# Zero-tile matmuls on TensorE ahead of and between the first transposes of an MLP kernel

## The chip, the cores and the metric

One core of a Trainium2 chip (trn2). The metric is device time in microseconds (us) of one execution, lower is better.

## The reference

A two-layer perceptron over 8192 tokens; the kernel computes in fp16 with fp32 accumulation.

```python
# x (8, 1024, 1024), w1 (1024, 4096), w2 (4096, 1024), all float32
def reference(x, w1, w2):
    h = x @ w1
    h = 0.5 * h * (1 + np.tanh(np.sqrt(2 / np.pi) * (h + 0.044715 * h ** 3)))
    return (h @ w2).astype(np.float32)
```

## The kernel before

Tokens are worked on in 8 superblocks of 1024 (`sb`). Each matrix product is split into 2x2 blocks and done with seven block products (Winograd's form of Strassen's scheme) instead of eight, so many operands are sums of blocks, made on DVE. In the first superblock everything has to be brought in: x arrives in fp32 and is transposed on TensorE; weights arrive in fp32 and are cast to fp16 by ACT and POOL.

```python
    def tt(out, in0, in1, op):                      # every sum on DVE comes from here (L111)
        nc.vector.tensor_tensor(out=out, in0=in0, in1=in1, op=op)
    # ... cut ...
        def load_cols(self, c, n):                  # first quad of w1, by columns
            cs = slice(c * P, (c + n) * P)
            kn = 2 * KH // n
            for b in range(2):
                cast = (nc.scalar.copy, pool_copy)[b]
                # ... cut: load fp32 weights into "gc", then cast(...)  (ACT L186, POOL L122)
    # ... cut ...
    def x_first():
        identity = consts.tile([P, P], F32, name="identity")
        make_identity(nc, identity)
        blocks = x_blocks()
        xs = XOps(blocks)
        for a in (1, 0):
            for q in range(NQ):
                # ... cut: load a [128 x 1024] fp32 tile xn of x
                for k in (1, 0):
                    ps = psum()
                    for j in range(KH):
                        nc.tensor.matmul(ps[:, j * P:(j + 1) * P],            # L244
                                         lhsT=xn[:, k, j * P:(j + 1) * P], rhs=identity,
                                         is_transpose=True, start=(j == 0), stop=(j == KH - 1))
                    # ... cut: copy ps to fp16, on DVE for k == 0, on ACT for k == 1 (L253)
            if a:
                xs.make(2)
        return xs
```

The first product, `matmul1`, runs seven products of four matmuls for each of 16 columns `c`. The same PSUM bank serves several products, with DVE and ACT reading it in between:

```python
        for c in range(NI):
            q, j = divmod(c, QC)
            # ... cut
            pb, qb = psum(), psum()
            product(pb, w, 4, True, False)          # each product: four 128x512 matmuls (L288)
            v = temp()
            nc.scalar.copy(out=v, in_=pb)           # L354
            product(qb, w, 5, True, False)
            u = temp()
            tt(u, v, qb, SUB)
            if late is not None:
                finish(*late)                       # product 6 of the column before
            rb = psum()
            product(rb, w, 1, True, False)
            s = temp()
            tt(s, u, rb, ADD)                       # must be read before product 7 adds to rb
            product(pb, w, 2, False, True)
            gelu("21", c, pb)                       # L298, ACT
            s2 = temp()
            tt(s2, s, pb, SUB)
            product(qb, w, 3, False, False)
            gelu("12", c, qb)
            product(rb, w, 7, False, True)
            # ... cut
            if j:
                ahead(q + 1, j)                     # operand sums of the next quad of columns
```

In the first two superblocks `ahead` makes the operand sums of the next quad on DVE, in steps:

```python
        def ahead(q, step):
            # ... cut: for sb > 1 the finished operands are loaded instead
            if step == 0:
                quad = MadeQuad(q, sb == 0)         # sb == 1: loads the blocks from raw_d
                quads.append(quad)
                # ... cut
            for m in ((), (4,), (1, 3), (7, 6))[step]:
                quads[q].sum(m)                     # one tt of 128x2048, then a store
            # ... cut
```

A scheduler orders the instructions of each engine when the program is built. In the first columns it puts products 4 and 5 of the second column ahead of product 3 of the first.

Of the kernel before, what the change touches and what calls it, by code (L numbers as in the profile page):

```python
# [9 lines left out]
DT = mybir.dt.float16  # L10
# [4 lines left out]
P = 128  # L15
# [41 lines left out]
def kernel(  # L57
# [7 lines left out]
    nc = tc.nc  # L65
# [3 lines left out]
    _, I = w1.shape  # L69
    _, O = w2.shape  # L70

    SB = 1024
    HT = SB // 2
# [4 lines left out]
    NQ = HT // P  # L78
# [9 lines left out]
    consts = ctx.enter_context(tc.tile_pool(name="consts", bufs=1))  # L88
# [12 lines left out]
    def psum():  # L101
        return pp.tile([P, HT], F32, name="ps")
# [4 lines left out]
    def unit(rows, cols):  # L107
        return up.tile([P, rows, cols], DT, name="u")
# [4 lines left out]
    def flat(t):  # L113
        return t.rearrange("p a b -> p (a b)")
# [3 lines left out]
    def load_in_order(out, in_, **kw):  # L118
        return tc.keep_in_program_order(nc.sync.dma_start(out=out, in_=in_, **kw))
# [108 lines left out]
    def x_blocks():  # L228
        return {b: unit(KH, HT) for b in ("22", "21", "12", "11")}

    def x_first():
        identity = consts.tile([P, P], F32, name="identity")
        make_identity(nc, identity)
        blocks = x_blocks()
        xs = XOps(blocks)
        for a in (1, 0):
            for q in range(NQ):
                r0 = a * HT + q * P
                xn = up.tile([P, 2, HT], F32, name="u")
                load_in_order(flat(xn), x2[r0:r0 + P, :])  # L240
# [3 lines that stand above are left out]
                        nc.tensor.matmul(  # L244
                            ps[:, j * P:(j + 1) * P],
                            lhsT=xn[:, k, j * P:(j + 1) * P],
                            rhs=identity,
                            is_transpose=True,
                            start=(j == 0),
                            stop=(j == KH - 1),  # L250
                        )
                    eng = nc.vector.tensor_copy if k == 0 else nc.scalar.copy
                    eng(  # L253
                        out=blocks[f"{a + 1}{k + 1}"][:, :, q * P:(q + 1) * P],
                        in_=ps.rearrange("p (j t) -> p j t", t=P),
                    )
            if a:
                xs.make(2)
        return xs
# [282 lines left out]
    def matmul2(sb, g):  # L542
# [69 lines left out]
                last = store(sb, b, q, c)  # L612
        return last

    warm = consts.tile([P, 1], F32, name="warm")
    nc.vector.memset(warm, 0.0)
    nc.scalar.activation(out=warm, in_=warm, func=GELU)
    xs = x_first()
    for sb in range(NSB):
        g, quad = matmul1(xs, sb)  # L620
# [39 lines left out]
```

## Time and profile before

| | |
|---|---|
| time, median of the first 3 runs | 1597.25 us (1596.09 to 1597.75) |
| span of the profiled run | 1593.6 us |
| TensorE (PE) busy | 1562.5 us, 98% |
| TensorE idle before 34 us | about 10 us |
| TensorE idle at 237 to 281 us | 9.0 us, in four waits |

The page of the profile of before gives busy time by engine and the chain that ended last: TensorE is the bottleneck as a whole.

```profile
PE 1562.5 (98%) x7872; PEld 774.8 (49%) x7872; DVE 945.6 (59%) x1203; ACT 485.2 (30%) x804; POOL 184.6 (12%) x270
...
PE 79%; DMA 2%; DVE 2%; issue 1%; ACT 0%; SPq 0%; DVEq 0%
```

The timeline of TensorE of before has the start, the length, and in brackets how long the engine was idle ahead of the entry and what ended that. Runs of matmuls without a pause are merged into one line.

```profile
4.42 5.58 PE L244 MATMUL ps<-identity,u 128*128 128x128 f32 x32 [4.42 <-DMA u<-in_x_dram]
...
17.62 1.04 PE L288 MATMUL ps<-u 128*128 128x512 f16 x4 [2.45 <-DVE u L111]
19.77 8.75 PE L288 MATMUL ps<-u 128*128 128x512 f16 x27 [1.12 <-POOL u L122]
29.30 4.26 PE L288 MATMUL ps<-u 128*128 128x512 f16 x19 [0.77 <-DVE tmp L111]
33.74 86.57 PE L288 MATMUL ps<-u 128*128 128x512 f16 x398 [0.18 <-DVE tmp L111]
...
244.81 32.48 PE L288 MATMUL ps<-u 128*128 128x512 f16 x136 [6.11 <-DVE tmp L111]
279.58 1.02 PE L288 MATMUL ps<-u 128*128 128x512 f16 x4 [2.30 <-DVE tmp L111]
```

After the transposes TensorE waits 2.45 and 1.12 us, then works with one short wait, and from 33.74 us it runs for 86.6 us without one. The two longest waits of the rest of the program end at 244.81 and 279.58 us (a wait of 2.16 us for a load ends at 1532.73 us).

The table of stretches of before, for TensorE (start:end, length, busy time and, in brackets, the matmuls that fall wholly or partly into the stretch, granted clock as a share of full speed, DMA share, GB/s; DMA packets are counted by their start, so that a share can read over 1):

```profile
18.00:20.00 2.00, 0.88 (x5) 0.64 1.19 294
20.00:22.00 2.00, 2.00 (x6) 0.50 1.03 311
22.00:24.00 2.00, 2.00 (x6) 0.50 1.09 371
24.00:26.00 2.00, 2.00 (x8) 0.66 0.97 289
```

The granted clock falls to 0.50 within the first line and comes back within the last; finer slices put the two changes at 18.55 and 25.38 us. At 20 to 24 us TensorE is busy all the time, with six matmuls in a stretch of 2 us.

Around it, the timeline of DVE and ACT of before:

```profile
19.75 6.20 DVE L111 TENSOR_TENSOR u<-u 128x512 f16<-128x512 f16 x11 [1.06 <-POOL u L122]
...
25.11 0.60 ACT L298 ACTIVATE g<-ps 128x512 f16<-128x512 f32 x1 [4.08 <-PE ps L288]
...
25.61 1.98 ACT L186 CAST u<-gc 128x1024 f16<-128x1024 f32 x2
25.88 0.67 DVE L111 TENSOR_TENSOR tmp<-tmp,ps 128x512 f32<-128x512 f32 x1
...
27.62 1.03 DVE L111 TENSOR_TENSOR u<-u 128x1024 f16<-128x1024 f16 x1 [1.06 <-ACT u L186]
...
28.57 0.68 DVE L111 TENSOR_TENSOR tmp<-tmp,ps 128x512 f32<-128x512 f32 x1
...
29.17 1.28 DVE L111 TENSOR_TENSOR u<-u 128x1024 f16<-128x1024 f16 x2
```

DVE makes eleven operand sums in one unbroken piece of 6.20 us. In its queue, the subtraction at 25.88 us comes after them and the addition at 28.57 us after another sum, which waits for two weight casts on ACT (25.61 us), which stand in ACT's queue behind a gelu (25.11 us), which waited for TensorE. TensorE's wait before 29.30 us is for that addition.

### The profile page before, as it was taken

How to read it: one execution, taken by the hardware profiler on the slowest of the kernel's cores; microseconds unless marked ns; L12 is line 12 of the kernel's file. 1: busy time of each engine (PE TensorE's matmuls, PEld its weight loads, DVE VectorE, ACT ScalarE, POOL GpSimd, SP SyncE). 2: the span in 40 equal slices, each digit the busy share in tenths (PEclk: the TensorE clock that was granted, in tenths of full speed). 3: DMA queues.
4: the chain of work that ended last, by engine and by line, in shares of the span. 5: the costliest groups of instructions: out<-in, count | busy, mean ns of one | idle time of the engine just before them, and what ended most of it. 6: DMA issues, size and time to landing. Idle time of an engine off the chain costs nothing.

```text
span 1593.6 us, 20478 instructions
## 1 busy us (share of the span) xinstructions
PE 1562.5 (98%) x7872; PEld 774.8 (49%) x7872; DVE 945.6 (59%) x1203; ACT 485.2 (30%) x804; POOL 184.6 (12%) x270
## 2 busy tenths in 40 slices
PE   7999998999999999999999999999999999999998
PEld 4444443444444455444554445544555445544455
DVE  6863245644755576555675557656475556655564
ACT  4644213431044301442114410244103430044200
POOL 2230113001310012000120001200012001200000
PEclk9999998999999999999999999999999999999999
DMA  9998999663994456845677346954469545663164
GB/s 305 349 297 292 274 388 357 188 241 115 359 320 133 185 223 246 273 104 198 245 273 233 115 178 245 331 184 171 154 244 364 153 163 198 243 244 133 53 223 173
DMA packets 169090, 365.22 MB, mean 229 GB/s; under 512 B 73120, under 2 KB 79264, under 8 KB 168096
## 3 DMA queue, kind: packets, MB, share of 16 engines
q1 hardware_dynamic: 152128, 297.84, 53.3%
q0 software_dynamic: 16864, 66.07, 12.6%
q8 instruction: 61, 1.00, 0.2%
q14 instruction: 37, 0.30, 0.1%
HBM read 285.21 MB, written 93.32 MB: 238 GB/s over the span
## 4 chain that ended last, share of the span: by engine, by line
PE 79%; DMA 2%; DVE 2%; issue 1%; ACT 0%; SPq 0%; DVEq 0%
PE ps L288 42%; PE ps L556 32%; PE ps L503 6%; DMA u<-w_d 1%; DVE u L111 1%; DMA u<-raw_d 1%; DVE tmp L111 0%; DMA u<-in_d 0%; DVE gc L111 0%; ACT tmp L585 0%; SPq L386 0%; DVEq L111 0%; SPq L492 0%
## 5 line engine op out<-in xcount | busy, mean ns | idle before, releaser
L288 PE MATMUL ps<-u 128*128 128x512 f16 x3584 | 782.2, 381 | 13.7 <-DVE tmp L111 9.9
L288 PEld LDWEIGHTS <-u 128*128 128x128 f16 x3584 | 351.9, 98 | 441.5 <-issue 19.8
L111 DVE TENSOR_TENSOR tmp<-tmp,ps 128x512 f32<-128x512 f32 x548 | 375.6, 687 | 312.7 <-ACT tmp L354 121.7
L556 PE MATMUL ps<-u,gc 128*128 128x512 f16 x1472 | 320.0, 379 | 0.0
L298 ACT ACTIVATE g<-tmp 128x512 f16<-128x512 f32 x256 | 161.1, 630 | 295.1 <-DVE tmp L111 295.1
L556 PEld LDWEIGHTS <-gc 128*128 128x128 f16 x1472 | 144.1, 98 | 173.6
L556 PE MATMUL ps<-u,g 128*128 128x512 f16 x896 | 195.7, 379 | 0.0
L111 DVE TENSOR_TENSOR u<-u 128x2048 f16<-128x2048 f16 (+2 forms) x130 | 133.8, 1067 | 87.8 <-ACT u L141 42.9
L298 ACT ACTIVATE g<-ps 128x512 f16<-128x512 f32 x256 | 152.2, 596 | 97.5 <-PE ps L288 97.3
L111 DVE TENSOR_TENSOR u<-u,ps 128x512 f32<-128x512 f32 x152 | 101.3, 682 | 83.3 <-ACT tmp L593 37.3
L386 POOL DMA_DIRECT2D out_dram<-tmp x72 | 39.2, 545 | 901.1 <-ACT tmp L585 723.8
L556 PEld LDWEIGHTS <-g 128*128 128x128 f16 x896 | 87.7, 98 | 104.4
L406 PE MATMUL ps<-u,g 128*128 128x512 f16 x512 | 111.2, 379 | 2.5 <-ACT tmp L451 2.5
L111 DVE TENSOR_TENSOR gc<-g,g 128x2048 f16<-128x2048 f16 x92 | 109.4, 1222 | 6.5 <-PE ps L556 6.5
L503 PE MATMUL ps<-u,gc 128*128 128x256 f16 x960 | 111.0, 274 | 0.8
L354 ACT COPY tmp<-ps 128x512 f32<-128x512 f32 x128 | 73.0, 570 | 104.0 <-PE ps L288 104.0
L503 PEld LDWEIGHTS <-gc 128*128 128x128 f16 x960 | 94.6, 99 | 13.4 <-issue 1.9
L111 DVE TENSOR_TENSOR gc<-u 128x2048 f16<-128x2048 f16 x60 | 73.2, 1220 | 39.2 <-PE ps L556 39.2
L111 DVE TENSOR_TENSOR tmp<-ps,tmp 128x512 f32<-128x512 f32 x128 | 88.4, 691 | 6.6 <-PE ps L288 1.9
L406 PEld LDWEIGHTS <-g 128*128 128x128 f16 x512 | 50.1, 98 | 63.4 <-issue 3.5
L111 DVE TENSOR_TENSOR u<-tmp,ps 128x512 f32<-128x512 f32 x28 | 19.3, 688 | 91.7 <-PE ps L556 80.4
L585 ACT COPY tmp<-ps 128x512 f32<-128x512 f32 x28 | 16.4, 587 | 177.3 <-PE ps L556 177.3
(33 smaller groups left out, 415.6 us busy)
## 6 DMA issues: line engine op xcount, KB each, us to landing
u<-w_d SPq DMA_DIRECT2D x316, 512.0 KB, 8.0
u<-in_d SPq DMA_DIRECT2D x84, 512.0 KB, 7.7
gc<-in_w_dram SPq DMA_DIRECT2D x64, 512.0 KB, 7.2
out_dram<-tmp POOLq DMA_DIRECT2D x72, 256.0 KB, 3.8
xb<-in_x_dram POOLq DMA_DIRECT2D x56, 256.0 KB, 11.2
w_d<-u SPq DMA_DIRECT2D x28, 512.0 KB, 6.5
w_d<-u POOLq DMA_DIRECT2D x28, 512.0 KB, 8.7
out_dram<-u POOLq DMA_DIRECT2D x40, 256.0 KB, 6.5
```

The costliest lines, as they stand in the source:

```text
L111: nc.vector.tensor_tensor(out=out, in0=in0, in1=in1, op=op)
L288: nc.tensor.matmul(bank, lhsT=ops[m][:, k, cs], rhs=xs[m][:, k, :], start=(first and k == 0), stop=(k == KH - 1), skip_group_check=not first,)
L298: gelu_last[0] = nc.scalar.activation(out=g[b][:, c, :], in_=src, func=GELU)
L354: nc.scalar.copy(out=v, in_=pb)
L386: return queue.dma_start(out=out2[r0:r0 + P, o0:o0 + OH], in_=src)
L406: nc.tensor.matmul(banks[i], lhsT=g[f"{i // NQ + 1}{a + 1}"][:, c, (i % NQ) * P:(i % NQ + 1) * P], rhs=w[a], start=(c == 0 and a == 0), st ...
L503: nc.tensor.matmul(bank[:, i * HO:(i + 1) * HO], lhsT=t[:, c, i * P:(i + 1) * P], rhs=y[j][:, c, :], start=(first and i == 0 and c == 0), ...
L556: nc.tensor.matmul(banks[q], lhsT=a[:, c, :], rhs=pieces[c // QC][:, c % QC, :], start=(first and c == 0), stop=(c == NI - 1), skip_group_ ...
L585: nc.scalar.copy(out=c21, in_=ps)
```

## The change

Intent: in before TensorE is idle for most of the time from 15.2 to 18.5 us, and its clock reads 0.50 from 18.55 to 25.38 us. Matmuls on a zero tile, whose result nobody reads, should keep it busy from the first microsecond and between the transposes, so that the transposes and the first real matmuls find the full clock.

```diff
+    def keep_clock(bank, n):
+        for _ in range(n):
+            tc.keep_in_program_order(
+                nc.tensor.matmul(bank, lhsT=idle[:, :P], rhs=idle, start=True, stop=True)
+            )
+
     def x_first():
         identity = consts.tile([P, P], F32, name="identity")
         make_identity(nc, identity)
+        idle_bank = psum()
+        keep_clock(idle_bank, 8)
         blocks = x_blocks()
@@ after the transposes and copies of each x tile @@
+                keep_clock(idle_bank, 2 if a or q < NQ - 1 else 6)
             if a:
                 xs.make(2)
@@ at the start of the program @@
+    idle = consts.tile([P, HT], DT, name="idle")
+    nc.vector.memset(idle, 0.0)
```

The program gains 28 matmuls (8, then 7 times 2, then 6) and one memset. The order of all other instructions on every engine, compared with the buffers' names mapped onto each other, is the same.

## The prediction

> **What bounds the kernel.** TensorE: the busy list gives PE 1562.5 us of 1593.6 (98%), the chain of waits ends 79% on PE. After 285 us the stage table shows PE full. The fillers touch the first 30 us. There, by timeline and half-microsecond windows:
>
> - 4.42 to 15.17 us: 64 fp32 transposes, fed by x tiles that land about every 1.3 us (DMA share 1.0). A transpose record averages 424 ns at 4 to 6 us and 276 ns at 12 to 14 us, the pitch going from about 0.21 to 0.133 us near 8.4 us: the array starts slow, although the clock column reads 1.00 there.
> - The clock column reads 0.50 from 18.6 to 25.35 us. Matmuls at 19.77 to 25.3 us stand 427 ns apart instead of 216.
> - [...]
>
> **What the change does.** Instruction order is otherwise identical. It adds 28 matmuls 128x512 (8 before the transposes, 2 after each of seven x tiles, 6 after the last), one small DVE memset, and holds one of 8 PSUM banks during the transposes. Costs (estimates from the spacings above): 28 x 0.216 = 6.0 us warm, up to twice that cold. The first 8 (about 3.4 us cold) fit almost wholly into the wait for x, ending about 4.6 us instead of 4.42. Then each tile costs 8 x 0.133 + 2 x 0.216 = 1.50 us on PE, more than the 1.3 us of its load: the transposes turn PE-bound and end at about 16.5 to 17.8 us, not 15.17, depending on when the clock rises.
>
> **How much is critical.** Twelve matmuls between 19.77 and 24.9 us gain about 2.5 us if warm. But PE's next product needs an operand sum on DVE, which runs without a pause from 19.75 to 25.95 us; it is ready only at about 24.6 us. So PE will wait from 22.3 to 24.6; most of the gain becomes idle time. What remains is indirect: gelu of the first product runs near 22.4 instead of 25.11 us, ACT's weight casts behind it (25.61 before) start about 1.5 us sooner, so do DVE's sum at 27.62 and the add that ends PE's wait at 29.30 us. Worth about 1.4 us. Later transposes push DVE's chain back 0.3 to 1.5 us, and the new wait at 22 to 24.6 us may let the clock fall again. Net at 34 us: 0.7 us sooner, give or take 1.5. PE is full from 34 to 122 us, and the loads of 125 to 280 us follow gelu, so I expect most of it to survive.
>
> **Prediction.** 1596.5 us, range 1594 to 1599.5; faster by over 2%: 0.01, within 2%: 0.98, slower: 0.01.
>
> **Signs.** Right: transposes at their short pitch before 8 us; last transpose after 16 us; clock 1.00 at 18.6 to 22 us; first products 216 ns apart; PE idle before the second column's first product, waiting for DVE; gelu near 22.5 us; everything after 34 us shifted by one constant, about a microsecond. Wrong: transposes still ending near 15.2 us, or clock 0.50 at 19 us.
>
> **What would break it.** [...]switching between fp32 transposes and fp16 fillers costing more than the sum; the stall at 238.7 to 244.8 us changing length; run-to-run spread (1596.09 to 1597.75) as large as the effect.

The sum came to 0.7 us sooner at 34 us, give or take 1.5.

## The result, and the profile after

| | before | changed |
|---|---|---|
| median of 4 runs | 1596.71 us (1596.09 to 1597.75) | 1596.28 us (1595.5 to 1598.14) |
| ratio | | 1.0002, 95% interval 0.9988 to 1.0016 |
| span of the profiled run | 1593.6 us | 1594.2 us |
| PE busy | 1562.5 us | 1567.3 us |

A ratio is the mean time of one kernel's fast runs over that of the other's fast runs of the same rounds, so it is not quite the ratio of the medians. The ratio in this table is that of before over changed, as the means show, 1596.82 and 1596.55 us; in the experiments below it is the kernel's time over that of before. Medians and means differ by 0.4 and 0.3 us in favour of the change, well inside the interval: no difference is shown. The page of the changed kernel:

```profile
PE 1567.3 (98%) x7900; PEld 775.8 (49%) x7900; DVE 948.7 (60%) x1204; ACT 485.0 (30%) x804; POOL 184.1 (12%) x270
```

The timeline of TensorE of the changed kernel (line numbers are 9 to 10 higher than in before; L235 is a filler). Entries that follow without a pause, the transposes and the other fillers among them, are left out, and so is the one at 90.10 us.

```profile
1.19 3.59 PE L235 MATMUL ps<-idle 128*128 128x512 f16 x8 [1.19 <-DVE warm L628]
...
18.33 1.04 PE L298 MATMUL ps<-u 128*128 128x512 f16 x4 [1.16 <-DVE u L111]
20.35 4.45 PE L298 MATMUL ps<-u 128*128 128x512 f16 x12 [0.98 <-POOL u L122]
25.25 7.70 PE L298 MATMUL ps<-u 128*128 128x512 f16 x34 [0.45 <-DVE u L111]
33.70 10.21 PE L298 MATMUL ps<-u 128*128 128x512 f16 x46 [0.75 <-DVE tmp L111]
44.67 44.93 PE L298 MATMUL ps<-u 128*128 128x512 f16 x205 [0.77 <-ACT tmp L364]
...
244.42 31.93 PE L298 MATMUL ps<-u 128*128 128x512 f16 x136 [5.26 <-DVE tmp L111]
279.76 20.50 PE L298 MATMUL ps<-u 128*128 128x512 f16 x86 [3.41 <-DVE tmp L111]
```

TensorE now has no pause from 1.19 to 17.17 us. Then it waits as before: 1.16 us for the first operand, 0.98 us for a POOL cast, and then 0.45 us for a sum on DVE. The unbroken piece of work starts at 33.70 us, where before it started at 33.74. And it is not unbroken any more: there are waits of 0.77 us before 44.67 and 0.50 us before 90.10 us. The two long waits are there too, 5.26 and 3.41 us.

The table of stretches of the changed kernel:

```profile
18.00:20.00 2.00, 1.04 (x4) 1.00 1.19 301
20.00:22.00 2.00, 1.65 (x5) 0.62 0.96 274
22.00:24.00 2.00, 2.00 (x7) 0.53 1.01 337
24.00:26.00 2.00, 1.55 (x8) 1.00 1.02 326
```

The clock was held past 18.55 us, where it fell before, but it fell at 20.47 us and came back at 23.89 us. The DVE and ACT timeline of the changed kernel:

```profile
20.33 6.21 DVE L111 TENSOR_TENSOR u<-u 128x512 f16<-128x512 f16 x11 [0.51 <-POOL u L122]
...
24.84 0.60 ACT L308 ACTIVATE g<-ps 128x512 f16<-128x512 f32 x1 [3.56 <-PE ps L298]
...
25.33 1.98 ACT L186 CAST u<-gc 128x1024 f16<-128x1024 f32 x2
...
27.35 0.69 DVE L111 TENSOR_TENSOR u<-u 128x1024 f16<-128x1024 f16 x1 [0.22 <-ACT u L186]
...
27.95 0.68 DVE L111 TENSOR_TENSOR tmp<-tmp,ps 128x512 f32<-128x512 f32 x1
...
28.55 1.53 DVE L111 TENSOR_TENSOR u<-u 128x1024 f16<-128x1024 f16 x2
```

The piece of eleven sums starts 0.6 us later than before and is as long; the gelu and the casts are 0.3 us earlier; the addition that TensorE waits for is 0.6 us earlier (27.95 for 28.57). By 33.7 us nothing is left of that.

### The profile page after: what moved, and what is told of

It is laid out like the page before. It is cut to its first block, busy times and chain, and to the rows that moved or that the text cites. A ratio compares the mean times of both kernels' runs of the same rounds, so it can differ in the third digit from the quotient of the medians.

```text
span 1594.2 us, 20535 instructions
## 1 busy us (share of the span) xinstructions
PE 1567.3 (98%) x7900; PEld 775.8 (49%) x7900; DVE 948.7 (60%) x1204; ACT 485.0 (30%) x804; POOL 184.1 (12%) x270
## 4 chain that ended last, share of the span: by engine, by line
PE 88%; DMA 7%; DVE 2%; ACT 1%; issue 1%; SPq 1%; POOL 0%; DVEq 0%; ACTq 0%
PE ps L298 46%; PE ps L566 32%; PE ps L513 6%; PE ps L416 3%; DMA gc<-in_w_dram 3%; DMA u<-w_d 2%; DVE u L111 1%; DMA u<-raw_d 1%; DMA w_d<-u 1%; ACT u L141 1%; SPq L119 0%; DMA u<-in_d 0%; DVE tmp L111 0%; DVE gc L111 0%; DMA u<-in_x_dram 0%
```

## The experiments

Every kernel below gave correct results. Time marks come from one profile each; the times from 5 or 6 runs a kernel. How coarse a mark is shows in the first stage: it ends (first matmul of the second product) at 120.2, 121.1, 122.4, 120.8 and 121.0 us in the five profiles of programs that work alike up to there, without fillers at the start (two of them have one memset more). The start of the long piece of work, which is TensorE's 51st product matmul, is as coarse: 33.74, 32.39, 34.52, 33.65 and 33.30 us in the same five, and 34.53 us in the profile of probe28, whose fillers come later.

Theory A: the first 34 us are paced by the sums on DVE and by weight loads, so the clock of TensorE there is worth next to nothing. Theory B: the clock was worth 2.5 us, but these fillers stop too early to hold it.

### The changed kernel again

> The changed kernel once more, unaltered. Theory A (the first matmuls are paced by the operand sums on DVE and by the weight loads, so their clock is worth next to nothing): total within 1 us of before. It also shows how far the time marks of one and the same kernel scatter. In the first profile of it the clock fell to 0.50 at 20.4 us and the second half of the first stage (first matmul of matmul2_first) began at 121.8 us, against 120.2 before. If those 1.6 us belong to the change, they come again; if they are chance, this mark lands anywhere between 119.5 and 122 us.

Measured: 1595.28 us median of 5 (1594.37 to 1596.48), before 1597.08 us (11 runs); ratio 0.9992, interval 0.998 to 1.0004. The end of the first stage came at 121.0 us, not 121.8; both lie inside what programs without the fillers show (120.2 to 122.4), so the 1.6 us of the first profile cannot be put down to the change. More telling: in this profile the clock did not fall at all in the first 36 us. Two stretches of it:

```profile
22.00:24.00 2.00, 0.52 (x3) 1.00 1.08 347
24.00:26.00 2.00, 0.94 (x5) 1.00 0.40 100
```

With the clock at 1.00, the 12 matmuls are done by 22.5 us, and then TensorE does nothing for 2.54 us. The timeline of TensorE of the same run:

```profile
25.06 7.69 PE L298 MATMUL ps<-u 128*128 128x512 f16 x34 [2.54 <-DVE u L111]
33.72 10.16 PE L298 MATMUL ps<-u 128*128 128x512 f16 x46 [0.97 <-DVE tmp L111]
```

The same kernel had a slow clock for 3.4 us in one run and none in another, and both times the long piece of work started at 33.7 us. That fits theory A, though one such mark proves little.

### No fillers between the transposes, 14 at the end (nm14)

```diff
-                keep_clock(idle_bank, 2 if a or q < NQ - 1 else 6)
+                keep_clock(idle_bank, 0 if a or q < NQ - 1 else 14)
```

> Fillers before the first transpose (8) and after the last (14), none between; the order of all other instructions is unchanged. Transposes should end near 15.0 us again, fillers run until about 18.2 us, and the clock should stay 1.00 through 16 to 23 us. Theory A: the matmuls from 19.7 to 22.3 us then run at full clock, TensorE waits until about 24.6 us for the sum on DVE, and the total stays within 0.8 us of before. Theory B (the fillers of the change stop too early, and a held clock would bring the 2.5 us that the slow matmuls cost): total 2 to 3 us under before and the mark of 120.2 us at about 117.7. The recorded prediction: about 1.4 us, by way of gelu and ACT's weight casts starting sooner.

Measured: 1595.94 us (1593.75 to 1596.28); ratio 0.9993, interval 0.9981 to 1.0005. The clock was 1.00 from 14 to 36 us. TensorE waited 2.13 us for a sum before 24.05 us, as theory A has it, and its long piece started at 33.09 us, 0.65 us sooner than before:

```profile
24.05 7.59 PE L298 MATMUL ps<-u 128*128 128x512 f16 x34 [2.13 <-DVE u L111]
33.09 86.76 PE L298 MATMUL ps<-u 128*128 128x512 f16 x398 [1.45 <-DVE tmp L111]
```

Theory B, which asked for 2 to 3 us, falls by the profile: the clock was held, TensorE waited for DVE all the same, and the first stage ended at 119.7 us, not near 117.7. (The total alone would not exclude 2 us.) The 0.65 us lie inside the scatter of that mark, and DVE's eleven sums began 0.62 us sooner in this profile as well (19.13 us), behind a POOL cast that had its weights sooner, so they are not shown to be the clock's. A cost that the prediction did not have shows in two lines of the timeline of this kernel, of DVE and of POOL:

```profile
27.66 2.13 DVE L111 TENSOR_TENSOR u<-u 128x1024 f16<-128x1024 f16 x2 [0.34 <-POOL u L122]
27.86 2.84 POOL L122 CAST u<-gc 128x1024 f16<-128x1024 f32 x2 [0.23 <-DMA gc<-in_w_dram]
```

The addition was 1.92 us sooner than before, the pair of 128x1024 sums 1.5 us sooner. But there it met two POOL casts, and took 2.13 us instead of 1.28; the casts took 1.42 us each instead of 1.04. In before POOL was idle for nearly all of that pair. Both records are longer while they run side by side; what the two contend for, the trace does not show.

### 14 at the end, with the fillers in between (last14)

```diff
-                keep_clock(idle_bank, 2 if a or q < NQ - 1 else 6)
+                keep_clock(idle_bank, 2 if a or q < NQ - 1 else 14)
```

> The changed kernel with 14 instead of 6 fillers after the last transpose, order otherwise unchanged. Transposes end at 15.9 us as in the changed kernel, fillers run to about 18.8 us, clock 1.00 until at least 23 us. Theory A: total within 0.8 us of before, DVE's long run of sums starts about 0.5 us later than before (20.3 against 19.75). Theory B: 2 us under before. If the delayed transposes are what eats a gain, this one is about 0.5 us slower than the version without fillers between the transposes.

Measured: 1595.52 us (1593.45 to 1597.36); ratio 0.9993, interval 0.9981 to 1.0005, the same as nm14. Here the clock held until 25.55 us and then fell until 28.96 us, after TensorE's new wait for DVE from 22.3 to 24.45 us. So four profiles with fillers had three different clocks (low at 20.5 to 23.9, low at 25.5 to 29.0, twice never low), and one time, within the scatter. Two expectations were missed: the last transpose ended at 15.08 us, not 15.9, and DVE's sums began at 19.53 us, not 20.3. So in this profile the transposes were not delayed, and it says nothing of what a delay costs.

### A known cost in the first stage (probe28)

```diff
+    def fill(bank, n, after):
+        with tc.issue_after(after.ins):
+            for _ in range(n):
+                last = tc.keep_in_program_order(
+                    nc.tensor.matmul(bank, lhsT=idle[:, :P], rhs=idle, start=True, stop=True)
+                )
+        return last
@@ in matmul1; product() now returns its last matmul, and the idle tile is made as in the change @@
             pb, qb = psum(), psum()
+            if sb == 0 and c == 12:
+                fill(pb, 28, p2)         # 28 zero-tile matmuls, placed after product 2 of c == 11
             product(pb, w, 4, True, False)
```

> Before, with 28 filler matmuls of 216 ns (6.05 us by the spacing of before) put in front of one product at about 95 us, where TensorE is busy without a pause; order otherwise unchanged. If a time gained or lost by TensorE in the first stage reaches the end in full, the total is 6.0 us over before, and the mark of 120.2 us becomes 126.2. If the loads of 125 to 280 us set the pace there and take up such shifts, the total is under 3 us over before.

Measured: 1600.73 us (1600.15 to 1603.66); ratio 1.003, interval 1.0018 to 1.0042, which is 4.8 us of 1597, between 2.9 and 6.7. The fillers are worth 6.05 us. So about four fifths of what TensorE loses late in the first stage reaches the end, between a half and all of it by the interval. The mark came at 128.1 us, not 126.2: 1.9 us too late, which is no more than the scatter of this mark. That a gain at that point would show as a loss does is argued, not shown; by their marks the kernels with fillers had none beyond the scatter to pass on.

### POOL's early casts moved to ACT, without and with a held clock (actcast, actcast_nm14)

```diff
-                cast = (nc.scalar.copy, pool_copy)[b]
+                cast = pool_copy if b and c == 0 else nc.scalar.copy
```

> Before, with one change: the weight casts of columns 1 to 3 that POOL did (two of 128x512 at 21.2 us, two of 128x1024 at 25.6 and 27.1 us) are done by ACT, which waits in that stretch; no fillers, so the slow clock from about 18.6 to 25.35 us stays. If the sums on DVE (11 from 19.75 to 25.95 us, mean 456 ns for a 128x512) are long because POOL casts run beside them, the same sums take 0.5 to 1 us less. With the clock low TensorE is not ready for them, so the total stays within 1 us of before.

> The same move of casts from POOL to ACT, with the 8 and 14 fillers of the version without fillers between the transposes, so that the clock is held at 1.00. Theory A, refined: once the clock is held, DVE sets the pace, and half of what it wins is lost again because its pair of 128x1024 sums runs beside POOL casts (2.13 us against 1.28 in the profile of before). Without those casts the pair takes about 1.3 us again, TensorE's unbroken stream starts at 31.9 to 32.6 us (33.09 with POOL casts, 33.74 before), and the total is 1 to 2 us under before. If DVE is not what paces it, the stream starts at 33.1 us as without the move.

Measured: actcast 1596.15 us (1594.62 to 1597.32), ratio 1.0006, interval 0.9994 to 1.0019; actcast_nm14 1596.18 us (1593.69 to 1597.04), ratio 1.0003, interval 0.999 to 1.0015; before, 1595.31 us (9 runs). The eleven sums took 5.38 us instead of 6.20 in both, so POOL's casts had cost them 0.8 us. With the clock held too, the pair of sums was short again. DVE of actcast_nm14, and TensorE of it:

```profile
27.35 1.29 DVE L111 TENSOR_TENSOR u<-u 128x1024 f16<-128x1024 f16 x2
```

```profile
32.53 10.16 PE L298 MATMUL ps<-u 128*128 128x512 f16 x46 [1.00 <-DVE tmp L111]
43.13 26.65 PE L298 MATMUL ps<-u 128*128 128x512 f16 x121 [0.44 <-ACT tmp L364]
```

The long piece started at 32.53 us, 1.2 us sooner than before and within the expected 31.9 to 32.6. In actcast, where the clock was low from 19.80 to 23.22 us, it started at 32.93 us, so the held clock is worth 0.40 us of this, and the mark scatters by 2 us. The collision is shown for this pair, though the pair after it, at 29.16 us, met POOL's next cast and took 2.13 us in its turn. The expected 1 to 2 us of total did not come: at 43.13 us TensorE waited 0.44 us for ACT's copy of a PSUM bank, and the first stage ended at 120.1 us, against 120.2 before (in actcast at 121.6). In ACT's queue that copy stands behind a cast that sat idle 1.88 us for weights from DRAM, in this run and, with 1.36 to 2.49 us, in the others. I read this as the weight loads taking back what the first 33 us win; the copy behind the cast is shown, but that the loads could not have come sooner is not. Nor does this wait account for all of it: the matmul that ends it was still 0.85 us ahead of the same one in before (43.13 and 43.98 us), and where the rest went between 44 and 120 us is open.

### Fillers in the long wait at 239 us (stall24)

```diff
-            product(qb, w, 3, False, False)
+            p3 = product(qb, w, 3, False, False)
+            if sb == 1 and c == 0:
+                fill(psum(), 24, p3)
```

> Before, with 24 fillers (5.2 us) in the long wait of TensorE at 238.7 to 244.8 us, where the clock falls to 0.50 and stays there until 250.7 us; nothing at the start of the program. If a filler pays where TensorE itself is what the next work waits for, the clock stays 1.00, the 14 slow matmuls after the wait go at 216 ns instead of 427, and the mark of 343.0 us (first matmul of the next stage) and the total come 2 to 3 us sooner. If the loads that end TensorE's next wait (at 277 to 280 us) set the pace, that wait grows by the same 2 to 3 us and the total stays within 0.8 us of before.

Measured: 1595.68 us (1594.97 to 1596.72), before 1595.31 us; ratio 1.0004, interval 0.9991 to 1.0018. This is the clean form of the question, because here the clock costs more (in before it was low for 10.24 us, from 240.42 us, against 6.83 us from 18.55 us): one stretch of before, then the same stretch of stall24.

```profile
246.00:248.00 2.00, 2.00 (x6) 0.50 1.03 418
```

```profile
246.00:248.00 2.00, 2.00 (x11) 1.00 1.02 414
```

At half clock six matmuls fall into these 2 us, with the clock held eleven. All of it was given back at TensorE's next wait, which was 2.30 us before (for an addition behind a sum that had waited 4.52 us for a load) and is now 5.29 us (in that wait the clock fell, and it was low from 280.26 to 283.68 us):

```profile
280.48 19.72 PE L296 MATMUL ps<-u 128*128 128x512 f16 x83 [5.29 <-DVE tmp L111]
```

The expected alternative came true. The load that this sum waits for was issued 2.1 us sooner than before (264.86 and 266.95 us), but it landed 0.9 us later (277.92 and 277.02 us), and the next stage began at 345.2 us, against 343.0 before. One load of x on POOL's queue also went ahead of a store here; what that did to the loads was not tried.

### The wait itself: sums behind the subtraction (unblock)

In before, DVE's queue at 239 us holds a sum for a later quad, waiting 5.30 us for a load, ahead of the addition that TensorE needs (244.07 us). DVE of before:

```profile
242.93 1.23 DVE L111 TENSOR_TENSOR u<-u 128x2048 f16<-128x2048 f16 x1 [5.30 <-DMA u<-raw_d]
244.07 1.46 DVE L111 TENSOR_TENSOR tmp<-tmp,ps 128x512 f32<-128x512 f32 x2
```

```diff
             for m in ((), (4,), (1, 3), (7, 6))[step]:
-                quads[q].sum(m)
+                if sb == 1 and q > 1:
+                    with tc.issue_after(s2_last[0].ins):   # the subtraction of the current column
+                        make_sum(quads[q].ops, m, quads[q].raw, KH, QW)
+                    nc.gpsimd.dma_start(out=w1_d[q][:, m - 1, :], in_=flat(quads[q].ops[m]))
+                else:
+                    quads[q].sum(m)
```

> Before, without fillers; in the second superblock the sums of the third and fourth quad on DVE are issued after the subtraction of the current column, because one of them, waiting 5.3 us for a load, stands in DVE's queue ahead of the addition that TensorE waits for at 238.7 us. If that order causes the 6.1 us wait, it shrinks to under 1 us, the clock does not fall at 240.5 us, and the mark of 343.0 us comes 3 to 9 us sooner, less what the wait at 277 to 280 us takes back. If the load itself is needed by the next column anyway, the wait only moves and the total stays within 1 us.

Measured: 1588.84 us (1587.45 to 1591.7), before 1595.31; ratio 0.9964, interval 0.9951 to 0.9976. Run again: 1591.25 us (1590.73 to 1592.53), before 1596.31; ratio 0.9971, interval 0.9959 to 0.9984.

> The reordered sums once more, as the partner of the next two: 5 to 8 us under before. In its first profile TensorE waited 4.76 us at 239.7 to 244.45 us, with the clock at 0.50 from about 243 to 249 us, and then not at all until 339.5 us.

The gain is real, but the expected reason is half wrong. The wait at 239 us did not shrink to under 1 us; it was 4.76 and 5.16 us in the two profiles, because behind the load stood another hold-up. TensorE and DVE of unblock:

```profile
244.45 95.10 PE L288 MATMUL ps<-u 128*128 128x512 f16 x428 [4.76 <-DVE tmp L111]
```

```profile
243.71 0.69 DVE L111 TENSOR_TENSOR tmp<-tmp,ps 128x512 f32<-128x512 f32 x1 [5.10 <-DMA out_dram<-tmp]
```

The addition now waits 5.10 us for a store of an earlier result, whose buffer it is to write. What went away is the wait at 280 us, where a sum waiting for a load had stood in the same way: after 244 us TensorE does not wait again until the next stage. The rest came from the wait at 239 us, shorter by 1.0 to 1.4 us, and from the slow clock after it, which lasted 6.8 us instead of 10.2. The next stage began 3.6 and 4.3 us sooner than before, within the expected 3 to 9. (The wait for the store was not tried further.)

### Fillers, once the next wait is gone (unblock_stall20, unblock_nm14)

The edit of stall24 with 20 fillers, and the edit of nm14, each on top of unblock.

> The reordered sums, with 20 fillers (4.3 us) in TensorE's wait of 4.76 us at 239.7 us. The same kind of filler gained nothing in the order of before, because the next wait, for loads at 277 to 280 us, grew from 2.3 to 5.3 us. Here that wait is gone, so the held clock should now reach the end: 13 matmuls at 216 instead of 427 ns, 2 to 2.8 us under the reordered sums alone (1586 to 1587 us if those take 1588.8). If a loads-bound wait comes back near 280 us, the two take the same time within 0.8 us.

> The reordered sums together with the fillers at the start (8 before, 14 after the transposes), that is the change's idea in its better form in a kernel that waits less. Theory A: whatever the first 33 us win (0.65 us in one profile) is less than the scatter that the weight loads put on the first stage (its end lay between 119.7 and 122.4 us in all profiles), so within 0.8 us of the reordered sums alone. If the old waits at 240 to 280 us were what swallowed the gain of the start, it shows here as 1 us or more.

Measured, in the same rounds as the second run of unblock (1591.25 us): unblock_stall20 1589.33 us (1588.11 to 1592.26), ratio to before 0.9961, interval 0.9947 to 0.9975; unblock_nm14 1590.31 us (1589.58 to 1593.16), ratio 0.9968, interval 0.9955 to 0.998. The means of five are 1591.4, 1589.7 and 1590.8 us. In the profile of unblock_stall20 the clock stays at 1.00:

```profile
246.00:248.00 2.00, 2.00 (x11) 1.00 1.04 422
```

TensorE of the same run, after the fillers:

```profile
244.32 92.80 PE L296 MATMUL ps<-u 128*128 128x512 f16 x428
```

The next stage begins at 337.0 us, against 339.4 and 338.7 us with the reordered sums alone, and TensorE has no wait in between. So the fillers that gained nothing before gain 1.7 us in the means here, a little under the expected 2 to 2.8; the intervals overlap, so the totals alone would not prove it, and the marks, 1.7 to 2.4 us apart, carry the scatter of the stages before. What supports it best is the length of this piece: from the first matmul after the wait to the next stage it takes 94.9, 95.0 and 94.9 us in unblock, its second run and unblock_nm14, where the clock is low for 6.8 us, and 92.6 us here. The fillers at the start change nothing beyond the scatter here either (0.6 us in the means, stage ends 121.1 and 120.8 us), so it was not the old waits at 240 to 280 us that hid their gain.

unblock_stall20 has the lowest ratio of the kernels tried, 0.39% under before.

## Why the prediction was right or wrong

The prediction's time, range and verdict were right: 1596.5 us predicted, 1596.28 us measured, no difference to before shown. There is luck in that: the range is 5.5 us wide, and no effect at all would have fallen into it too. Its small net gain of about 0.7 us is within what the runs cannot tell apart. Step by step:

- **TensorE would wait for DVE once its matmuls were fast.** Right, and the core of it. Predicted: idle from 22.3 to 24.6 us. Measured where the clock held: idle from 22.5 to 25.06 us (the changed kernel, again) and from 21.9 to 24.05 us (nm14). This wait is where the 2.5 us went. One distance shows it: from the start of DVE's eleven sums to TensorE's 17th product matmul, the one that ends this wait, it is 4.91 or 4.92 us in nine profiles, with and without fillers, however long the clock was low. In the profiles of before and probe28 it is 5.12 us, so at this point the slow clock had cost 0.20 us and no more. Shorter sums move it: 4.09 us in actcast_nm14.
- **Transposes end at 16.5 to 17.8 us.** Wrong; the last ended at 15.88 us. The failed term is the "8 x 0.133" of a tile. The 0.133 us came from dividing the length of a group of eight, 1.06 us, by eight; but that length holds the whole record of the last one, 0.273 us, while the starts stood 0.109 us apart. Tiles followed each other 1.305 us apart, so after 0.43 us for two fillers, eight transposes take 0.87 us. They were busy without pause all the same, and the delay was 0.7 us. Even that came with the slow start. In before the starts of the first 19 transposes stood 0.213 us apart (the first two 0.239 us), and 0.109 us within a group of eight from 8.41 us on, with the clock column at 1.00 throughout. In last14, with the same fillers in between, the transposes stood 0.109 us apart from 5.1 us on, in the changed kernel only from 7.0 us, and in last14 the last one ended at 15.08 us.
- **Clock 1.00 at 18.6 to 22 us.** Not in the first profile (down at 20.47 us), yes in the second. That the clock differs from run to run should have been the expectation. The fillers end at 17.2 us. In the first profile waits of 1.16 and 0.98 us for DVE and POOL follow; in the second it had one wait of 1.57 us. How busy TensorE must be for the clock to hold is not shown.
- **Gelu near 22.5 us, casts 1.5 us sooner, the addition sooner.** Right when the clock held: gelu at 22.56 us, first cast at 23.45 us for 25.61, addition at 27.76 us for 28.57.
- **"Worth about 1.4 us", net 0.7 us at 34 us.** Not shown. The changed kernel had 0.04 and 0.02 us at the start of its long piece, its best form 0.65 us, and all of it lies inside the scatter of that mark without fillers, 32.39 to 34.53 us. A term that the sum lacked is the collision of DVE's sums with POOL's casts, 0.85 us on one pair (2.13 for 1.28 us). That it ate the gain is not shown: with those casts taken away the held clock brought 0.40 us (actcast_nm14 against actcast), less than the 0.65 us with them.
- **"I expect most of it to survive."** Not decided. In actcast_nm14 1.2 us at 33 us were gone at the end of the stage, by marks that scatter by 2 us each. Losses late in the stage do survive (probe28, 4.8 of 6.05 us); the prediction took a gain early in it for the same thing, and no run shows that. By the totals the three kernels with fillers that ran in the same rounds (after_again, nm14, last14) took 1595.6 us in the mean of 16 runs, before 1596.5 us in that of 11: 0.9 us less, with a 95% interval, worked out from these runs, of about -0.2 to 2.1 us. So the predicted 0.7 us is neither shown nor excluded.

Left open: why the first stage ends anywhere from 119.7 to 122.4 us in programs that do the same work, and whether the weight loads of 34 to 45 us could be brought forward.

## What to carry to other kernels

In this kernel, holding TensorE's clock was worth something only where TensorE's own work set the pace up to the next stage: find the next wait first, and see what ends it. The same kind of filler gave nothing at 239 us while a load ended the wait at 280 us, and about 2 us after that wait was gone (1.7 us in the means, 2.3 us in the profile). And look at what stands ahead in an engine's queue (in before the addition at 244.07 us came after a sum that had waited 5.30 us for a load): moving sums that wait for loads behind the ones TensorE needs gave about 5 us (ratios 0.9964 and 0.9971), more than any filler.
